# Laying a planned instruction order with 140 stored shifts of its due times

## The chip, the cores and the metric

One NeuronCore of a Trainium2 chip runs the whole program. The metric is the device time of one execution in microseconds (us). The program has five instruction queues that run on their own and meet through semaphores: TensorE (PE, with its weight loads as PEld), VectorE (DVE), ScalarE (ACT), GpSimd (POOL) and SyncE (SP), which here issues nearly all DMA transfers.

## The reference

One layer of a decoder with three groups of heads, 1024 tokens of 2048 channels, float32:

```python
h = rmsnorm(x, ln_g)
proj = h @ w_in                                   # columns split among the groups
(g_u, g_v, g_z, d_q, d_k, d_v, d_z, d_a, d_b, c_q, c_z) = split(proj)
out_a = gmlp_spatial_gating(g_u, g_v, ...) * silu(g_z)          # 4 groups of 128, chunks of 128
q, k, v = split(causal_conv_silu(concat(d_q, d_k, d_v)))
o = gated_delta_rule(l2norm(q), l2norm(k), v, g, beta)          # 8 heads of 128, chunked
out_b = rmsnorm(o, dn_norm_g) * silu(d_z)
mk, mv = split(rmsnorm(mem, mem_norm_g) @ w_mem_kv)             # 256 memory tokens
out_c = softmax(c_q @ mk.T / sqrt(128)) @ mv * silu(c_z)        # 4 heads of 128
x = x + concat(out_a, out_b, out_c) @ w_out
return rmsnorm(x, final_g)
```

## The kernel before, in words

Tokens are handled in two halves of 512, channels in 16 blocks of 128. The two large projections (into the heads, `project_stage`, and out of them, `out_pair`) are done as block products with seven instead of eight multiplications (`seven`): sums and differences of halves of the activations and of the weights are made first, and products are combined afterwards. Float32 accuracy comes from splitting each operand into a rounded high part and a remainder (`split_to`: a cast on ACT, a subtraction on DVE) and multiplying three times (`triple`). In the profile the high and low parts of the weights are `rhi` and `rlo`, those of the activations `lh` and `ll` or `lm`, loaded weights are `raw` and `kept`, PSUM banks are `acc` and `dn`, results copied out of them `obs`, `yu` and `yz`.

In order of time: the memory's keys and values are projected and `x` is normed and turned (to about 80 us); the head projections run from there to about 1250 us, and between their products lie the delta rule's convolution, inverse and scan (`front`, `inverse`, `levels`, `scan_step`), the spatial gating (`spatial`, `gmlp`) and the attention (`attend`); the output projection runs to the end, with the final norm in `close`.

None of this order is the order of the program text. Every call such as `PE.matmul` or `Q.dma_start` goes through an `Engine` and is stored by `Plan.add` as an `Op` with its engine, its estimated cost (`price`), the operations that must wait for it (`succ`) and a class from `rank(...)`. Classes under zero mark the first loads. PE operations given inside `together()` have one head, `lead`, and follow it as its `tail`. At the end `Plan.issue` decides the order and calls the stored functions in it, which puts them on the engines' queues. That is why the profile gives line 398, the call in `issue`, for every instruction.

Three functions make the order:

- `lay(key, hold)` plays the operations through a model of the engines. At each step the engine that is free first takes, among its ready operations, the one with the smallest key. It writes each operation's planned start into `o.at` and returns the planned end. DMA transfers go one after another at `DMA_RATE` bytes a nanosecond after the issue, and land `DMA_FIXED` nanoseconds later; SyncE may not run more than `AHEAD` nanoseconds ahead of them. On ACT an operation that needs another function table is put back by `hold`.
- `late(preds)` plays the same operations backwards from the last layout and returns for each the latest start (negative, counted back from the end) that still keeps the end, with distances lengthened by `STRETCH`. These are the keys, the deadlines, of the next `lay`.
- `issue` starts with the classes as keys, alternates `lay` and `late` for `PASSES` rounds, keeps the layout with the smallest planned end, sorts the operations by it and issues them.

Keys and times in the plan are nanoseconds.

Of the kernel before, what the change touches and what calls it, by code (L numbers as in the profile page):

```python
# [53 lines left out]
class Engine:  # L54
    def __init__(self, plan, eng, ns):
        self.plan, self.eng, self.ns = plan, eng, ns
# [6 lines left out]
class Plan:  # L63
# [3 lines left out]
    DMA_RATE = 350.0  # L67
    DMA_FIXED = 3800.0
    SWITCH = 250.0
    FIRST, SPREAD, PASSES, STRETCH, AHEAD = 0, 1.75, 8, 1.25, 1000.0  # L70
    TABLE, HOLD = 1300.0, 6000.0

    def __init__(self, nc):
        self.ops = []
# [247 lines left out]
    def late(self, preds):  # L322
# [56 lines left out]
                    heapq.heappush(soon[lead.eng], (ready[lead.idx], lead.idx))  # L379
        return goal  # L380

    def issue(self):
        preds = [[] for _ in self.ops]
        for o in self.ops:
            for s in o.succ:
                preds[s.idx].append(o)
        best = None
        key, hold = [o.cls for o in self.ops], 0.3
        for n in range(self.FIRST + self.PASSES + 1):
            end = self.lay([o.cls * 1.0e9 + o.idx if o.cls < 0 else k for o, k in zip(self.ops, key)], hold)  # L390
            if best is None or end < best[0]:
                best = end, [o.at for o in self.ops]
            key, hold = self.latest() if n < self.FIRST else self.late(preds), self.HOLD
        for o, o.at in zip(self.ops, best[1]):
            pass
        self.ops.sort(key=lambda o: (o.at, o.idx))
        for o in self.ops:
            o.fn(*o.args, **o.kw)  # L398
# [1523 lines left out]
```

## Time and profile before

| | |
|---|---|
| median of 3 runs | 1594.31 us (1592.87 to 1595.48) |
| the profiled execution's own time | 1593.81 us |
| its span, first to last instruction | 1592.1 us |
| instructions | 24568 |
| PE matmuls | 8349, busy 1570.2 us |
| DVE, ACT, POOL busy | 1228.7, 963.3, 106.7 us |
| mean granted PE clock | 0.997 |
| DMA | 434.12 MB, mean 273 GB/s |

Busy time counts the instructions' own time on an engine. Matmuls overlap each other, and their ends are modelled, so a PE that is busy all the time is not for that reason at its highest pace. Idle time of an engine matters only where the work that ends last waits for it. In the rows of stretches the columns are the stretch, its length, then busy time and, in brackets, number of instructions of PE, PEld, DVE, ACT and POOL, the granted clock of PE as a share, the mean busy share of the 16 DMA engines and what they moved.

### The profile page before, as it was taken

Reading aid. Unit: us, or ns where it says so; the run is one execution under the profiler, and the core shown is the slowest. Engines: PE = TensorE matmul, PEld = TensorE weight load, DVE = VectorE, ACT = ScalarE, POOL = GpSimd, SP = SyncE. Lnnn points to the kernel's source line nnn. Section 1 sums busy time; section 2 is a strip of 40 time slices with the busy share of each in tenths; the row PEclk is TensorE's granted clock in tenths of the full one; section 3 lists DMA queues with packets and bytes.
Section 4 is the critical chain, followed back from the end, with each engine's and each line's share of the span. In section 5 each row is a group of like instructions: output and inputs, shape, how many; then the busy total and the mean of one; then the engine's idle time right before and its main releaser. Section 6 shows DMA issues by size and latency. Waiting matters only on the chain.

```text
span 1592.1 us, 24568 instructions
## 1 busy us (share of the span) xinstructions
PE 1570.2 (99%) x8349; PEld 1315.3 (83%) x8349; DVE 1228.7 (77%) x1818; ACT 963.3 (61%) x2006; POOL 106.7 (7%) x143
## 2 busy tenths in 40 slices
PE   8999999999999999999999989999999999999997
PEld 7988888888887888888888878888888888888886
DVE  6977655877589997777789996867658888688875
ACT  6833255535698436787886557765658864344455
POOL 0100010001000100111111001000000000000001
PEclk9999999999999999999999999999999999999999
DMA  9999966888679898786888988999877989778647
GB/s 320 327 317 346 284 171 183 294 292 245 218 246 315 298 325 254 257 250 205 282 281 277 303 244 245 341 325 309 268 245 253 298 298 347 235 263 293 232 146 276
DMA packets 335951, 434.12 MB, mean 273 GB/s; under 512 B 70089, under 2 KB 160466, under 8 KB 335826
## 3 DMA queue, kind: packets, MB, share of 16 engines
q1 hardware_dynamic: 334098, 429.39, 83.3%
q0 software_dynamic: 1088, 2.10, 0.4%
q8 instruction: 66, 1.08, 0.3%
q10 hardware_dynamic: 640, 1.07, 0.2%
q14 instruction: 59, 0.48, 0.1%
HBM read 332.78 MB, written 99.16 MB: 271 GB/s over the span
## 4 chain that ended last, share of the span: by engine, by line
PE 92%; ACT 3%; DMA 2%; DVE 1%; issue 1%; SPq 0%; POOL 0%; POOLq 0%; ACTq 0%; DVEq 0%
PE acc L398 56%; PE dn L398 35%; ACT jk L398 1%; ACT rhi L398 1%; DMA h0d<-tn 1%; SPq L398 0%; DMA tn<-vd 0%; DMA ut<-in_x_dram 0%; DMA kept<-in_mem_dram 0%; DVE rlo L398 0%; DMA raw<-in_w_in_dram 0%; DVE vs L398 0%; ACT vs L398 0%; DVE tn L398 0%; ACT inv L398 0%
## 5 line engine op out<-in xcount | busy, mean ns | idle before, releaser
L398 PE MATMUL acc<-lh,rhi 128*128 128x512 f32 x1024 | 396.2, 396 | 2.9 <-DVE obs L398 1.2
L398 PE MATMUL acc<-lh,rlo 128*128 128x512 f32 x1024 | 382.9, 397 | 0.0
L398 ACT CAST rhi<-raw 128x1024 fp32r<-128x1024 f32 (+1 forms) x148 | 186.6, 1261 | 248.8 <-PE dn L398 133.8
L398 DVE TENSOR_TENSOR rlo<-raw,rhi 128x1024 fp32r<-128x1024 f32 (+1 forms) x148 | 219.3, 1482 | 109.0 <-ACT rhi L398 98.8
L398 PE MATMUL acc<-ll,rhi 128*128 128x512 f32 x688 | 268.0, 395 | 0.8 <-DVE ll L398 0.8
L398 PEld LDWEIGHTS acc<-lh,rhi 128*128 128x128 f32 x1024 | 192.3, 188 | 41.1 <-issue 1.5
L398 PEld LDWEIGHTS acc<-lh,rlo 128*128 128x128 f32 x1024 | 191.9, 188 | 37.4
L398 DVE TENSOR_TENSOR ll<-ll,lh 128x1024 fp32r<-128x1024 f32 x122 | 148.5, 1217 | 17.3 <-ACT lh L398 17.0
L398 PEld LDWEIGHTS acc<-ll,rhi 128*128 128x128 f32 x688 | 129.6, 189 | 26.4 <-DVE ll L398 1.3
L398 ACT CAST lh<-ll 128x1024 fp32r<-128x1024 f32 x122 | 128.2, 1051 | 29.5 <-PE dn L398 9.0
L398 PE MATMUL acc<-lm,rhi 128*128 128x512 f32 x336 | 130.6, 394 | 0.0
L398 PE MATMUL dn<-lh,rhi 128*128 128x512 f32 x288 | 112.6, 393 | 0.0
L398 PE MATMUL dn<-lh,rlo 128*128 128x512 f32 x288 | 109.7, 393 | 0.0
L398 DVE TENSOR_TENSOR raw<-raw,kept 128x1024 f32<-128x1024 f32 (+1 forms) x56 | 80.9, 1444 | 6.9 <-DMA raw<-in_w_in_dram 5.9
L398 DVE TENSOR_TENSOR rlo<-kept,rhi 128x1024 fp32r<-128x1024 f32 (+1 forms) x29 | 41.8, 1443 | 47.3 <-ACT rhi L398 44.4
L398 PE MATMUL dn<-ll,rhi 128*128 128x512 f32 x192 | 75.2, 393 | 0.0
L398 PEld LDWEIGHTS acc<-lm,rhi 128*128 128x128 f32 x336 | 63.2, 188 | 11.9
L398 ACT CAST rhi<-kept 128x1024 fp32r<-128x1024 f32 (+1 forms) x29 | 35.6, 1229 | 50.3 <-PE dn L398 26.2
L398 PEld LDWEIGHTS dn<-lh,rhi 128*128 128x128 f32 x288 | 54.1, 188 | 10.6
L398 PEld LDWEIGHTS dn<-lh,rlo 128*128 128x128 f32 x288 | 54.0, 188 | 10.5
L398 POOL TENSOR_TENSOR hs<-hs,mhalf 128x4 f32<-128x4 f32 x32 | 48.4, 1515 | 195.3 <-DVE hs L398 194.9
L398 POOL TENSOR_TENSOR small<-small,mhalf 128x1 f32<-128x1 f32 x26 | 21.6, 832 | 562.8 <-DVE small L398 562.8
(421 smaller groups left out, 3449.6 us busy)
## 6 DMA issues: line engine op xcount, KB each, us to landing
raw<-in_w_in_dram SPq DMA_DIRECT2D x120, 512.0 KB
ll<-hsd SPq DMA_DIRECT2D x54, 512.0 KB
raw<-in_w_out_dram SPq DMA_DIRECT2D x48, 512.0 KB
raw<-in_w_in_dram SPq DMA_DIRECT2D x72, 256.0 KB
lm<-hsd SPq DMA_DIRECT2D x26, 512.0 KB
pd<-obs SPq DMA_DIRECT2D x48, 256.0 KB
late<-os SPq DMA_DIRECT2D x44, 256.0 KB
kept<-in_w_in_dram SPq DMA_DIRECT2D x20, 512.0 KB
```

The lines of the kernel that those rows point to most:

```text
L398: o.fn(*o.args, **o.kw)
```

## The change

`PASSES` goes from 8 to 16, so the loop in `issue` makes 17 layouts instead of 9 and keeps the best of them, now with its keys. These keys are then changed by `nudged`, and one more `lay` with the changed keys gives the order that is issued. `fixed` is what stood in the loop before: operations of a class under zero keep the key of their class.

`nudged` goes through the 140 stored numbers `NUDGES` in order. A number's top bits are its kind, the rest seeds a small generator (`draw`). Kind 0 picks a stretch of the kept layout (a start, and a length from `WIDTHS`), a reach from 256 to 32768 ns and a share, and adds to the key of that share of the stretch's operations a random amount of that scale, up or down. Kind 1 picks one operation and takes the reach off its key and off those of its ancestors that lie within half a width before it. Kind 2 picks one operation and adds the reach to its key and to those of its heirs within half a width after it. Heads of PE bundles stand for their bundles. The numbers were chosen beforehand, under layouts with late transfers; the kernel itself only applies them. No operation, buffer or dependency is added or removed.

```diff
-    FIRST, SPREAD, PASSES, STRETCH, AHEAD = 0, 1.75, 8, 1.25, 1000.0
+    FIRST, SPREAD, PASSES, STRETCH, AHEAD = 0, 1.75, 16, 1.25, 1000.0
     TABLE, HOLD = 1300.0, 6000.0
+    WIDTHS = (4.0e3, 8.0e3, 16.0e3, 24.0e3, 40.0e3, 60.0e3, 90.0e3, 140.0e3)
+    NUDGES = (
+        26298409, 11320507, 8404763, 7722074, 16576787, 19920401, 40970024, 17359656, 9019627,
...
+        10043970, 4847855, 34621008,
+    )
...
+    def fixed(self, key):
+
+        return [o.cls * 1.0e9 + o.idx if o.cls < 0 else k for o, k in zip(self.ops, key)]
+
+    def nudged(self, preds, end, at, key):
+
+        key = list(key)
+        heads = sorted((at[o.idx], o.idx) for o in self.ops if o.lead is o and o.cls >= 0)
+        for n in self.NUDGES:
+            kind, s = n >> 24, n & 0xFFFFFF
+
+            def draw():
+                nonlocal s
+                s = (s * 1664525 + 1013904223) & 0xFFFFFFFF
+                return s >> 8
+
+            draw(), draw()
+            if kind:
+                t0, i = heads[int(draw() / 2.0**24 * len(heads))]
+                width = 0.5 * self.WIDTHS[draw() >> 21]
+                reach = 2.0 ** (8 + (draw() >> 21))
+                seen, todo = {i}, [i]
+                while todo:
+                    o = self.ops[todo.pop()]
+                    key[o.idx] += -reach if kind == 1 else reach
+                    for x in (o, *o.tail):
+                        for q in preds[x.idx] if kind == 1 else x.succ:
+                            q = q.lead
+                            near = at[q.idx] > t0 - width if kind == 1 else at[q.idx] < t0 + width
+                            if q.idx not in seen and q.cls >= 0 and near:
+                                seen.add(q.idx)
+                                todo.append(q.idx)
+                continue
+            first = draw() / 2.0**24 * end
+            last = first + self.WIDTHS[draw() >> 21]
+            reach = 2.0 ** (8 + (draw() >> 21))
+            share = ((draw() >> 21) + 1) / 16
+            for t, i in heads[bisect.bisect_left(heads, (first, -1)) :]:
+                if t >= last:
+                    break
+                if draw() / 2.0**24 < share:
+                    key[i] += reach * (draw() + draw() + draw() - 1.5 * 2.0**24) / 2.0**23
+        return key
...
-            end = self.lay([o.cls * 1.0e9 + o.idx if o.cls < 0 else k for o, k in zip(self.ops, key)], hold)
+            end = self.lay(self.fixed(key), hold)
             if best is None or end < best[0]:
-                best = end, [o.at for o in self.ops]
+                best = end, [o.at for o in self.ops], key
             key, hold = self.latest() if n < self.FIRST else self.late(preds), self.HOLD
-        for o, o.at in zip(self.ops, best[1]):
-            pass
+        self.lay(self.fixed(self.nudged(preds, *best)), self.HOLD)
```

More of the change, by code (lines that the diff above doesn't have):

```diff
@@ L1 @@
+import bisect
 import heapq
```

14 rows, old and new, of the table NUDGES are left out of this document.

## The prediction

> **What bounds the kernel now.** The page comes first: shares of busy time, then the chain that ended last.
>
> ```profile
> span 1592.1 us, 24568 instructions
> PE 1570.2 (99%) x8349; PEld 1315.3 (83%) x8349; DVE 1228.7 (77%) x1818; ACT 963.3 (61%) x2006; POOL 106.7 (7%) x143
> PE 92%; ACT 3%; DMA 2%; DVE 1%; issue 1%; SPq 0%; POOL 0%; POOLq 0%; ACTq 0%; DVEq 0%
> ```
>
> TensorE (PE) is busy in 99% of the span and is 92% of the chain. The change adds no matmul and takes none away, so only time in which PE is not working at its pace can be won. 1592.1 less 1570.2 leaves 21.9 us idle. The second view says where: busy time of each engine by stretch (length, then PE, PEld, DVE, ACT, POOL, granted clock, DMA share, GB/s).
>
> ```profile
> core 0: us, PE busy (x) PEld busy (x) DVE busy (x) ACT busy (x) POOL busy (x), PEclk, DMA share, GB/s
> 0.00:2.90 2.90, 0.01 (x1) 0.04 (x1) 0.00 (x0) 1.19 (x1) 1.39 (x10) 1.00 0.28 62
> 2.90:12.00 9.10, 6.95 (x27) 5.53 (x28) 3.36 (x8) 4.08 (x9) 0.00 (x0) 1.00 0.87 274
> 12.00:64.00 52.00, 52.00 (x356) 47.66 (x355) 43.77 (x74) 45.65 (x97) 6.14 (x7) 1.00 1.02 351
> 64.00:80.00 16.00, 14.89 (x120) 13.98 (x120) 14.44 (x31) 12.59 (x30) 1.44 (x3) 1.00 1.00 308
> 80.00:440.00 360.00, 360.00 (x1649) 298.32 (x1648) 241.09 (x279) 165.23 (x253) 22.25 (x31) 1.00 0.83 261
> 440.00:520.00 80.00, 78.35 (x405) 64.75 (x404) 70.42 (x136) 72.68 (x221) 6.64 (x8) 1.00 0.88 285
> 520.00:880.00 360.00, 359.84 (x2150) 303.06 (x2149) 300.60 (x504) 242.85 (x624) 40.33 (x47) 1.00 0.83 269
> 880.00:919.00 39.00, 37.85 (x170) 31.14 (x168) 36.07 (x60) 19.72 (x25) 2.45 (x2) 1.00 0.95 296
> 919.00:934.00 15.00, 12.05 (x43) 8.97 (x44) 14.41 (x35) 7.53 (x10) 0.59 (x1) 0.89 0.97 289
> 934.00:1000.00 66.00, 65.21 (x416) 54.12 (x414) 49.22 (x81) 45.56 (x94) 8.49 (x12) 1.00 0.83 249
> 1000.00:1320.00 320.00, 319.94 (x1868) 270.20 (x1869) 247.95 (x365) 219.71 (x473) 11.47 (x15) 1.00 0.89 292
> 1320.00:1582.00 262.00, 262.00 (x1157) 216.91 (x1156) 204.34 (x248) 123.14 (x169) 4.41 (x7) 1.00 0.75 253
> 1582.00:1592.10 10.10, 1.11 (x5) 0.57 (x4) 3.06 (x6) 3.39 (x6) 1.08 (x2) 0.65 0.75 277
> ```
>
> Read each row as length less PE: 2.89, 2.15, 0, 1.11, 0, 1.65, 0.16, 1.15, 2.95, 0.79, 0.06, 0 and 8.99, together 21.9. The first two are the wait for the first loads, the last is the final rows' norm and stores. In between lie 7.87 us in five places. The third view names what PE waited for there (total, times, longest).
>
> ```profile
> PE dn L398 <- DMA y<-in_mem_norm_g_dram: 2.9, 1, 2.9
> PE dn L398 <- DVE raw L398: 1.6, 1, 1.6
> PE dn L398 <- DMA gr<-in_ln_g_dram: 1.3, 1, 1.3
> PE acc L398 <- DVE obs L398: 1.2, 1, 1.2
> PE acc L398 <- DVE ll L398: 0.8, 1, 0.8
> PE dn L398 <- DMA tn<-vd: 0.8, 1, 0.8
> PE acc L398 <- ACT yu L398: 0.8, 1, 0.8
> PE dn L398 <- DVE tn L398: 0.6, 1, 0.6
> ```
>
> Outside the start every one is a single event: VectorE (DVE) late with obs, raw and ll around 919 to 934, where it is busy 14.41 of 15 us; ScalarE (ACT) late with yu in 440 to 520, where it is busy 72.68 of 80; a reload of tn just before 1000. Neither engine lacks time in the whole, only there. That is what an order can mend: in 80 to 440 DVE has 119 us free and ACT 195.
>
> The worst place costs a second time.
>
> ```profile
> 926.00:930.00 4.00, 1.50 (x6) 0.85 (x6) 4.00 (x14) 1.05 (x1) 0.36 (x1) 0.96 1.01 247
> 930.00:933.20 3.20, 3.20 (x10) 2.55 (x10) 3.04 (x7) 1.05 (x1) 0.00 (x0) 0.51 0.96 330
> ```
>
> After PE had worked 1.50 of 4 us, its granted clock was 0.51 for 3.2 us. Over the 15 us row the clock is 0.89, so 0.11 by 15 = 1.65 us are lost while PE counts as busy. [...]
>
> **The change part by part.**
>
> *What runs on the chip.* Nothing is added. `issue`, `fixed`, `nudged` and `lay` run while the program is built; the same operations, buffers and dependencies come out, in another order on each queue. Compute work stays at 1570.2 us of PE, 1228.7 of DVE, 963.3 of ACT. One exception: an order can change how often ACT reloads its table.
>
> ```profile
> L398 ACT ACT_TABLE_LOAD x23 | 29.5, 1283 | 2.7 <-PEq L1908 1.7 <-DVE small L398 0.6
> ```
>
> Five loads more or fewer are 6.4 us of ACT, hidden while ACT is at 61%; in 440 to 520, with 7.3 us free, two more would still fit. I put 0.
>
> *Twice as many passes (8 to 16).* The loop keeps the pass with the lowest end by the planner's own reckoning, so the base may be another order altogether. The trace can't show it. Bounds: if no later pass is better, 0; otherwise anything that reordering can do, which is the next step's range.
>
> *The 140 nudges.* By their top bits 69 shift a stretch's operations at random, 45 pull an operation and its ancestors forward, 26 push an operation and its heirs back, by 256 to 32768 ns. Decoded with the generator in `nudged`, 14 of the 69 stretches begin in the first tenth of the plan, 32 between two and four tenths (about 320 to 640 us), 8 between five and six. So they stand densest where the rows show 1.11 and 1.65 us idle, thinner where 4.1 (1.15 and 2.95) are. Each moved operation takes its DMA issue along, and SyncE's queue works in order:
>
> ```profile
> SPq L398 <- PE dn L398: 203.7, 121, 5.4
> SPq L398 <- DVE rlo L398: 145.2, 90, 5.2
> SPq L398 <- PE acc L398: 122.3, 67, 4.9
> ```
>
> It waits anyway, up to 5.4 us at a time, for PE to free a buffer. A load put behind such a wait comes later, one put ahead earlier. POOL, busy 7%, hides its own moves.
>
> *What can be won.* The loads at the very start have a negative class, which `fixed` keeps as before: 2.89 and 2.15 stay. The last 8.99 is a chain of norm and stores behind the last matmul: stays. Left: 1.11 + 1.65 + 0.16 + 1.15 + 2.95 + 0.79 + 0.06 = 7.87 idle, plus 1.65 of half clock: 9.5 us. That is the upper end, since no row shows more; the lower end is a loss, as new stalls can open (priced below). Of the 9.5 I take 60%, 5.7: the DVE knot at 919 to 934 is the largest piece and has slack before it, but 14.41 of 15 us busy means that a whole stretch must move, not one operation. Where it goes, the next late thing is ACT's or DVE's casts in the same crowded stretches.
>
> *Sum.* The profiled execution took 1593.81 us (span 1592.1 plus 1.7 around it), 0.5 below the median 1594.31. 1593.81 - 5.7 = 1588.1; I say 1588.
>
> [...]
>
> **The rivals.** A difference of 0.2%, 3.2 us, is about what a measurement can tell from none.
>
> *A, the forecast (0.54):* the knots at 440 to 520 and 880 to 934 open mostly, nothing as large closes. Gains from 3.2 to 9.5: 1584 to 1591.
>
> *B, nothing to see (0.24):* the order mends what its plan shows, not what the chip does. The stalls are single events of under 1.7 us, and the nudges' densest stretches hold 1.11 and 1.65 idle: 2.8 us even if both go, so 1591 to 1597. Against it: the 4.1 us at 880 to 934 sit on DVE load, which a plan can see.
>
> *C, slower (0.18):* a weight load for the output projection (1320 to 1582, no idle now) slips behind waits of SyncE's queue. Each slip of its longest wait is 5.4 us of idle PE, plus half of 3.2 us at half clock, 1.6: 7.0. DVE has 58 us free there and can't make a late load good. One slip with A's gain of 5.7 gives 1595; it decides once losses exceed 5.7 + 3.2 = 8.9, so from two slips: 14.0 - 5.7 = 8.3, near 1602. Against it: DMA is at 0.75 in that stretch, and `lay` lets SyncE issue only while less than 1 us of transfers is queued (`AHEAD`), a rule that stays.
>
> *D, more than the idle (0.04):* time hidden in "busy" shrinks too. 12 to 64 is 52 us with no idle, yet DVE 43.77 and ACT 45.65 pace it and the chain runs through ACT and DVE there. If ACT's 45.65 set it alone, 6.4 us would go as well: 1593.8 - 9.5 - 6.4 = 1578.
>
> **How the numbers follow.** Forecast 1588, own range 1584 to 1591. The range for 8 in 10 takes in B whole and the lower part of C, down to beyond A's upper gain: 1580 to 1600. Faster is A + D, 0.58; the same is B, 0.24; slower is C, 0.18.
>
> **What would show it.** Right: PE busy within 3 us of 1570, span shorter, PE idle between 12 and 1582 us under 4; no wait of PE on DVE raw, obs or ll over 0.5 us; granted clock 1.00 throughout 12 to 1582. B: the idle total between 5 and 10, in other places. C: idle or a half clock in 1320 to 1582 on a DMA wait. Wrong altogether: a changed count of matmuls, or PE's busy time moving by more than its idle.

## The result and the profile after

The changed kernel takes 1585.74 us in the median of 5 runs (1582.74 to 1587.86), the kernel before 1594.31 (1592.87 to 1595.9, now 5 runs). The ratio is 0.9946, 95% interval 0.9934 to 0.9957: 8.6 us or 0.54% faster. The profiled execution took 1585.74 us and spans 1584.0, 8.1 less than before.

From the page of the changed kernel, span, busy time and the chain that ended last:

```profile
span 1584.0 us, 24571 instructions
PE 1568.0 (99%) x8349; PEld 1316.2 (83%) x8349; DVE 1229.7 (78%) x1818; ACT 965.3 (61%) x2004; POOL 98.5 (6%) x143
PE 98%; issue 0%; DMA 0%; DVE 0%; SPq 0%; ACT 0%; POOLq 0%; POOL 0%; DVEq 0%
```

The matmuls are as many as before. PE's idle time fell from 21.9 to 16.0 us (5.9 of the 8.1), its busy time from 1570.2 to 1568.0 (the other 2.2). The chain is now 98% PE.

The same stretches as before, of the changed kernel (the last two end 8 us earlier; those not shown, 12 to 64, 80 to 440 and 1000 to 1320, have no idle time of PE):

```profile
2.90:12.00 9.10, 6.56 (x23) 5.00 (x24) 3.56 (x9) 4.09 (x9) 0.00 (x0) 1.00 0.87 308
64.00:80.00 16.00, 16.00 (x137) 15.87 (x136) 15.90 (x30) 12.32 (x33) 1.48 (x2) 1.00 1.03 314
440.00:520.00 80.00, 80.00 (x408) 67.52 (x407) 73.68 (x127) 70.73 (x202) 7.20 (x9) 1.00 0.86 280
520.00:880.00 360.00, 359.74 (x2155) 303.20 (x2154) 303.73 (x518) 247.93 (x640) 33.43 (x46) 1.00 0.85 274
880.00:919.00 39.00, 39.00 (x177) 32.30 (x177) 37.77 (x64) 23.08 (x31) 2.03 (x2) 1.00 0.99 309
919.00:934.00 15.00, 15.00 (x73) 12.42 (x73) 14.21 (x35) 6.26 (x7) 1.71 (x2) 1.00 0.95 285
934.00:1000.00 66.00, 64.00 (x478) 53.34 (x477) 49.06 (x77) 45.56 (x100) 7.40 (x12) 0.98 0.83 239
1320.00:1574.00 254.00, 254.00 (x1123) 210.38 (x1122) 196.17 (x238) 117.23 (x157) 4.09 (x7) 1.00 0.76 251
1574.00:1584.00 10.00, 1.68 (x8) 1.07 (x6) 3.15 (x6) 3.40 (x6) 0.64 (x2) 0.82 0.78 285
```

Four of the five places with idle PE are clean: 64 to 80, 440 to 520, 880 to 919, 919 to 934. The fifth, 934 to 1000, has 2.00 us instead of 0.79. PE's waits say with what:

```profile
PE dn L461 <- DMA y<-in_mem_norm_g_dram: 2.9, 1, 2.9
PE acc L461 <- DVE ll L461: 2.0, 1, 2.0
PE dn L461 <- DMA gr<-in_ln_g_dram: 1.0, 1, 1.0
PE dn L461 <- DMA kept<-in_mem_dram: 0.9, 1, 0.9
```

Three of the four are first loads. The new one, DVE late with `ll`, stands at 994 to 996, and its origin is a load. Stretches of time there, then SyncE's issues (start, duration of so many issues), then DVE's instruction that waited:

```profile
980.00:984.00 4.00, 4.00 (x29) 3.65 (x29) 3.16 (x7) 1.48 (x4) 0.00 (x0) 1.00 0.40 97
992.00:996.10 4.10, 2.11 (x55) 1.24 (x53) 3.58 (x4) 3.04 (x8) 0.00 (x0) 1.00 1.08 391
996.10:999.60 3.50, 3.50 (x10) 2.73 (x11) 3.50 (x5) 2.36 (x5) 0.00 (x0) 0.60 1.00 310
```

```profile
972.10 3.79 SPq L461 DMA_DIRECT2D sm<-gvd  x4
975.99 4.13 SPq L461 DMA_DIRECT2D vd<-sm  x4
984.70 0.41 SPq L461 DMA_DIRECT2D raw<-in_w_in_dram  x1
992.52 1.23 DVE L461 TENSOR_TENSOR raw<-kept,raw 128x1024 f32<-128x1024 f32 x1 [4.47 <-DMA raw<-in_w_in_dram]
994.80 1.22 DVE L461 TENSOR_TENSOR ll<-ll,lh 128x1024 fp32r<-128x1024 f32 x1
```

SyncE spends 7.9 us from 972.1 on eight issues. In the 4 us behind them the DMA engines' share is down to 0.40. The weight load of 984.70 comes after these eight and eight more. DVE waits 4.47 us for the load, two operations of 1.2 us (`raw` and `rlo`) then stand ahead of `ll`, and PE is idle for 2.0 us. After it the granted clock is 0.60 for 3.5 us. In the kernel before, the half clock stood in 930 to 933.

**Where the time went, by equal work.** A row's idle time does not tell how fast PE is inside "busy". So I gave each matmul about the spacing that its shape shows in the trace where nothing holds it up (0.227 us for 512 columns, 0.105 for 128; the medians over either whole trace are 0.227 and 0.109), summed these in order of time, and compared when the two kernels reach equal sums. After minus before, for the stretches between these times of before:

| stretch of before | after minus before | its idle and half clock before |
|---|---|---|
| start to 20 us | +1.3 | 2.89 + 2.15 (first loads) |
| 50 to 90 | -2.2 | 1.11 |
| 90 to 440 | +0.3 | 0 |
| 440 to 520 | -3.2 | 1.65 |
| 520 to 880 | +0.1 | 0.16 |
| 880 to 950 | -6.9 | 1.15 + 2.95 + 1.65 of clock |
| 950 to 975 | -0.6 | part of 0.79 |
| 975 to 1015 | +3.2 | rest of 0.79 |
| 1015 to the last matmul | +0.6 | 0.06 |
| behind the last matmul | -0.7 | 8.99 |

Together -8.1. The three knots (50 to 90, 440 to 520, 880 to 950) gave 12.3 us, where their rows showed 8.5. The rest of the gain, 3.8, was slow pace counted as busy. The table is an estimate that hangs on the spacings: with the 1st to the 50th percentile of each shape's spacings in the two traces, the three knots come to 12.3 to 13.0, 440 to 520 alone to -3.1 to -3.9, and 975 to 1015 to 2.8 to 4.8.

The slow pace can also be seen without these weights. A matmul of 512 columns is drawn 0.39 us long, while the next one can start 0.227 us after it, so a short wait disappears under the modelled end of the matmul before it. The weight loads show such waits. Here are the longest of PEld's in 440 to 520 of the kernel before; they are 4.1 us in all, where PE's row shows 1.65 idle:

```profile
PEld acc L398 <- ACT yu L398: 1.2, 1, 1.2
PEld acc L398 <- ACT obs L398: 0.9, 2, 0.8
PEld dn L398 <- ACT os L398: 0.7, 1, 0.7
PEld dn L398 <- DVE ai L398: 0.5, 1, 0.5
```

The changed kernel has none there. Over 50 to 90, 440 to 520 and 880 to 934, the weight loads waited 11.8 us before (2.0 + 4.1 + 5.7) and not at all after; PE's rows showed 6.9 of it.

The 1.3 us lost at the start are 0.4 us of idle time and, for the larger part, pace: matmuls of 256 columns in a row start 0.21 us apart until 11.5 us in the kernel before and until 13.7 in the changed one, and 0.12 apart afterwards. Experiment 9, with the order of the kernel before there, changes pace at 10.3, so this point moves between executions.

### The profile page after: what moved, and what is told of

The parts are those of the page before. It is cut to its first block, busy times and chain, and to the rows that moved or that the text cites. A ratio compares the mean times of both kernels' runs of the same rounds, so it can differ in the third digit from the quotient of the medians.

```text
span 1584.0 us, 24571 instructions
## 1 busy us (share of the span) xinstructions
PE 1568.0 (99%) x8349; PEld 1316.2 (83%) x8349; DVE 1229.7 (78%) x1818; ACT 965.3 (61%) x2004; POOL 98.5 (6%) x143
## 4 chain that ended last, share of the span: by engine, by line
PE 98%; issue 0%; DMA 0%; DVE 0%; SPq 0%; ACT 0%; POOLq 0%; POOL 0%; DVEq 0%
PE acc L461 60%; PE dn L461 38%; DMA kept<-in_mem_dram 0%; SPq L461 0%; DVE rlo L461 0%; DVE ll L461 0%; ACT obs L461 0%; DVE kd L461 0%; DVE vs L461 0%; POOLq L1980 0%; POOL small L461 0%; DVE kT L461 0%; DVE small L461 0%; ACT sm L461 0%; DVEq L461 0%
## 5 line engine op out<-in xcount | busy, mean ns | idle before, releaser
L461 PE MATMUL acc<-lh,rhi 128*128 128x512 f32 x1024 | 390.1, 396 | 0.0
L461 PE MATMUL dn<-rlo,lh 128*128 128x512 f32 x144 | 56.1, 389 | 0.0
L461 PE MATMUL dn<-rhi,ll 128*128 128x512 f32 x144 | 56.1, 389 | 0.0
```

## The experiments

All kernels are compared with runs of the kernel before on the same chip (medians 1594.5 to 1595.6).

**1 and 2. The shifts applied to one part of the time only.** `nudged` returns the shifted keys before 550 us of the plan and the unshifted ones behind it, or the other way round.

```diff
-        key = list(key)
+        old, key = key, list(key)
...
-        return key
+        return [k if t < 550.0e3 else o for k, t, o in zip(key, at, old)]    # e1_early
+        return [k if t >= 550.0e3 else o for k, t, o in zip(key, at, old)]   # e2_late
```

> The nudges' shifts are kept only for operations that the kept layout starts before 550 us; the others have their old keys. Theory T (each knot is opened in its own place): the gains up to 560 us of the changed kernel stay (0.4 us lost at the start, 1.1 us idle gone at 64 to 80, 1.65 us idle and about 1.5 us of stretched pace gone at 440 to 520), about 3.7 us in all, and the knot at 880 to 934 is there as before (some 4 us idle and one half clock): 1589 to 1592 against 1594.3, span 3 to 5 us shorter. Rival U (the gain comes from the layout as a whole): the half alone gives nothing, within 2 us of before.

> The other half: shifts only for operations that the kept layout starts at or after 550 us. Theory T: PE idle at 440 to 520 stays at about 1.65 us and at 64 to 80 at 1.1, the knot at 919 to 934 (2.95 us idle, 1.65 us of half clock, 1.15 idle just before) is gone, 4 to 7 us, less 2 to 3.6 us if the new stall near 992 us comes with it: 1587 to 1591. Rival U: within 2 us of before.

The early half gives 1591.68 us, ratio 0.9987 (0.9976 to 0.9997), the late half 1593.3, 0.9989 (0.9979 to 0.9999): 2.8 and 1.2 us of the 8.6. But each half opens its own knots just as the whole does. Of the early half, two stretches:

```profile
440.00:520.00 80.00, 80.00 (x407) 67.44 (x406) 73.22 (x127) 70.80 (x202) 7.21 (x9) 1.00 0.86 280
520.00:880.00 360.00, 356.67 (x2140) 300.04 (x2140) 301.01 (x511) 245.84 (x640) 36.73 (x46) 1.00 0.84 270
```

By equal work it has -2.2 in 50 to 90 and -3.2 in 440 to 520, as the whole change has, and then +3.8 in 520 to 880, most of it in waits of PE between 640 and 760 (3.3 us). The late half keeps its knots before 550 and gains 5.2 at 880 to 950, then loses 3.3 and 2.4 behind 975. Its median fits the rival, within 2 us of before, and only its trace fits the theory. This trace has to be read with care: its execution took 1596.97 us, 3.7 over the median, and it also lost 3.0 us between 50 and 160, where PE's order is the same, matmul by matmul, as in the kernel before.

So the knots are untied locally, but the gain is not a sum of parts: behind 550 us, where shifted and unshifted keys meet, the early half has stalls in 520 to 880 (+3.8) that the full set has not (+0.1), and the late half loses more behind 975 (5.7) than the full set does (3.8). How much of the late half's loss is chance of one execution is not shown. The knots themselves repeat: idle time in 440 to 520 is 1.65 us before and 1.64 in the late half and in experiment 9, which have the same order there.

**3. The same kinds and number of shifts, from other seeds.**

```diff
-            kind, s = n >> 24, n & 0xFFFFFF
+            kind, s = n >> 24, (n + 3) & 0xFFFFFF
```

> The same 140 kinds, with 3 added to each seed, so other places and other shifts of the same spread of sizes. Theory T (the stored numbers fit the places that they were chosen for): shifts of up to 32 us put loads and splits past their deadlines, PE idle grows from 16 us to 40 or more, 20 to 45 us slower than before, 1615 to 1640, with waits of PE on DVE, ACT and DMA all over. Rival V (any shuffle of a tight layout loosens its knots): within 5 us of before, some knots gone and others new.

1637.78 us, ratio 1.0266 (1.0252 to 1.028), 43 us slower. Its largest wait of PE:

```profile
PE acc L461 <- ACT lh L461: 10.7, 9, 2.3
```

So the gain does not come from shuffling as such. Only one other set of seeds was tried. Whether a set unlike the 140 can gain as much is not shown: those of experiments 7 and 8 hold some 130 of the old numbers.

**4. The late load of 984.70.** Three SyncE operations that hold it up are laid behind it; the rest of the order stays.

```diff
         self.lay(self.fixed(self.nudged(preds, *best)), self.HOLD)
+        for n, i in enumerate((8651, 9013, 7710)):
+            self.ops[i].at = self.ops[9067].at + 1.0 + n
```

> The changed kernel, with one block moved on SyncE's queue alone: the weight load of raw that was issued at 984.70 us goes ahead of three issues that stood before it (a store of obs, a load of ll, a load of kT; 1 MB together). Theory T (the new stall at 992 to 996 us is SyncE's: its queue had fallen 4 us behind, at a DMA share of 0.40 in 980 to 984): the load lands 3 to 4 us earlier, DVE's wait of 4.5 us for it shrinks to under 1, PE's 2.0 us idle on ll goes and with it the half clock, 2 to 3.6 us less than the changed kernel, 1582 to 1584. Rival W (the transfers themselves are the limit there, share 1.00 and over in 984 to 996): the wait moves to ll, kT or tn, within 1 us of the changed kernel, PE idle in 984 to 1000 still 1.5 to 2.5.

1584.49 us, ratio 0.9933 (0.992 to 0.9947), which can't be told from the changed kernel. In the profile the wait on `ll` is gone and no half clock follows, but another 1.0 us of idle time opens (a stretch, SyncE's issues, DVE's instruction that had waited, PE's waits):

```profile
996.00:1000.00 4.00, 2.95 (x14) 2.19 (x14) 3.57 (x5) 3.56 (x8) 0.00 (x0) 1.00 1.06 385
```

```profile
976.78 4.55 SPq L463 DMA_DIRECT2D vd<-sm  x4
984.34 0.40 SPq L463 DMA_DIRECT2D raw<-in_w_in_dram  x1
989.19 1.22 DVE L463 TENSOR_TENSOR raw<-kept,raw 128x1024 f32<-128x1024 f32 x1
```

```profile
PE dn L463 <- issue: 1.3, 2, 1.0
```

The load is issued only 0.36 us earlier by the clock, because this execution is 1.4 us later at that place (the eight issues begin at 973.46 instead of 972.10). But it is there when DVE asks for it: DVE starts at 989.19 without a wait, 4.85 us after the issue, where the changed kernel's DVE got the load 7.82 us after the issue (984.70 to 992.52) and that of experiment 5 7.6 us after. So without the three transfers (1 MB) ahead of it the load is there some 3 us sooner after its issue. By equal work 975 to 1015 costs +1.4 over before instead of +3.2. So this load is the origin of the stall as far as one profile shows it; what it is worth in the median stays open, since the next run shows how much this place moves by itself.

**5. The changed kernel again, unaltered**, beside the next three.

> The changed kernel once more, unaltered, so that the other three of this group are compared with it on one chip. Every theory: 0.4 to 0.7% under the kernel before, about 1585.7; PE idle between 12 and 1574 us near 2.3, the wait on ll near 992 to 996 there again.

1584.93 us, 0.9941 (0.9929 to 0.9952). Its profiled execution, the slowest of the five (1587.74), shows the same instructions in other stalls: PE is idle for 4.59 us between 12 and 1574, not the 2.3 that was expected (PE's waits, then the stretches at 992 to 1000):

```profile
PE acc L461 <- DVE ll L461: 2.1, 2, 1.7
PE acc L461 <- ACT yu L461: 1.3, 1, 1.3
```

```profile
992.00:996.00 4.00, 3.40 (x61) 2.30 (x59) 2.48 (x3) 3.56 (x10) 0.07 (x1) 1.00 1.10 377
996.00:1000.00 4.00, 2.60 (x10) 1.80 (x11) 4.00 (x5) 2.50 (x7) 0.00 (x0) 1.00 1.01 317
```

The stall on `ll` is there again, with DVE waiting 4.13 us for the same load but no half clock behind it, and 1.3 us of `yu` appear behind it. The three knots are as in the first profile: -2.2, -3.2 and -6.4. A difference of 1 to 2 us in one place of one profile is therefore no evidence, while the knots, which repeat, are.

**6. One shift of the 140 left out**, the last, of the kind that pushes an operation and its heirs back.

```diff
-        10043970, 4847855, 34621008,
+        10043970, 4847855,
```

> The changed kernel without the last of its 140 nudges; the plan's own end goes from 1572.3 to 1581.3 us, the difference lying at 430 to 570 us. Theory T (a nudge has its worth only with all others in place, as each later layout hangs on every earlier choice, and the chip follows the plan): the gain at 440 to 520 goes or a new wait of 2 to 6 us opens at 520 to 600; 3 to 9 us slower than the changed kernel, 1588 to 1594. Rival X (the plan's stalls at 430 to 570 are for the most part its own, since the kernel before ran past 1.9 us of them at 560): within 2 us of the changed kernel.

1592.33 us, 0.9987 (0.9979 to 0.9996): 7.4 us slower than the changed kernel on the same chip, for one number. Stretches, and PE's longest waits between 400 and 620:

```profile
440.00:520.00 80.00, 79.09 (x403) 66.36 (x402) 72.20 (x121) 70.77 (x204) 3.71 (x6) 1.00 0.89 284
520.00:880.00 360.00, 358.02 (x2137) 299.57 (x2136) 300.39 (x510) 244.22 (x630) 37.55 (x48) 1.00 0.84 270
919.00:934.00 15.00, 15.00 (x72) 12.47 (x71) 15.00 (x32) 8.21 (x11) 0.59 (x1) 1.00 1.02 315
```

```profile
PE dn L461 <- DVE lm L461: 1.0, 1, 1.0
PE acc L461 <- DVE ll L461: 0.9, 2, 0.8
PE dn L461 <- ACT os L461: 0.9, 1, 0.9
```

The knots at 50 to 90 and 880 to 950 stay untied (-2.1, -6.9), but 90 to 440 takes 1.3 us more than in the changed kernel, 440 to 520 1.4 and 520 to 880 3.4. By equal work all of it, some 6 us, arises between 400 and 600. So the last shift closes small waits for ACT and DVE that the other 139 leave there.

**7 and 8. More shifts, chosen to bear lateness better**: 330 and 352 numbers in `NUDGES` in place of 140, most of the old ones among them, nothing else altered.

> The changed kernel with 330 nudges instead of 140, most of the new ones picked so that the issued order loses less when transfers land late and SyncE's issues take longer; the plan's own end stays (1572.6 for 1572.3). Theory R (of the plan's 15.5 us the chip gave 8.1 in the profile, because transfers and issues came later than planned, above all at 992): PE idle between 12 and 1574 us under 1, no half clock there, 2 to 5 us under the changed kernel, 1580.5 to 1584. Rival Y (what is left is pace and the plan's own pessimism in the kernel before, not lateness): within 1.5 us of the changed kernel.

> As the one before, with another set of 352 nudges, picked in the same way from other draws; the plan's own end is 1572.3. Theory R: the same gain, 2 to 5 us under the changed kernel, since it is the slack against lateness that counts and not these numbers. Rival Y: within 1.5 us of the changed kernel. If one of the two sets gains and the other doesn't, neither holds as stated, and the difference is in single stalls.

1587.39 us, 0.9953 (0.9941 to 0.9965), and 1587.1, 0.9949 (0.9937 to 0.996). No gain over the changed kernel (1584.93); the intervals overlap. PE's idle time between 12 and 1574 us is 2.67 (the row below) and 2.72, where the changed kernel had 2.27 and 4.59 in two executions:

```profile
12.00:1574.00 1562.00, 1559.33 (x8320) 1307.52 (x8320) 1223.17 (x1804) 954.79 (x1990) 93.80 (x132) 1.00 0.85 274
```

The theory expected less than 1 us idle, and that did not come about either. So these two sets did not pay; whether lateness still costs something in the changed kernel is not settled by them.

**9. The worst knot by itself.** In the kernel before, without any shift, four products on DVE at 925.87 to 928.24 (`raw` from `dn` times `utri`), for which PE waited 1.65 us, are laid together ahead of the 1.2 us subtraction for `rlo` that came before them.

```diff
         for o, o.at in zip(self.ops, best[1]):
             pass
+        for n, i in enumerate((7356, 7357, 7358, 7359)):
+            self.ops[i].at = self.ops[8709].at - 1.0 + 0.1 * n
```

> The kernel before, with one edit on DVE's queue alone: the four products raw<-dn,utri, on which PE waited 1.65 us at 928.30, stand together ahead of the 1024-wide split that came before them, as they stand together in the changed kernel. Theory K (the order of these four was the knot): PE's wait on DVE raw goes, and with less idle the half clock at 929.7 to 933.1 too; PE idle in 919 to 934 falls from 2.95 to about 1.3, 1.6 to 3.3 us less than before, 1591 to 1593. Theory S (the knot is a stretch: DVE is 14.41 of 15 us busy there, and the matmul behind these waits for ll, which DVE can't give before 929.6 us as long as ACT's cast of lh begins only at 926.28): the wait moves to ll and grows to 2.5 to 3.5 us, PE idle in 919 to 934 stays between 2.3 and 3.5, within 1 us of before.

1594.62 us, 0.9996 (0.9987 to 1.0005): no change. The profile shows where it went. Of this kernel, the four products on DVE, the cast on ACT and the subtraction on DVE that make `ll`, PE's wait, the stretch:

```profile
923.38 0.85 DVE L400 TENSOR_TENSOR raw<-dn,utri 128x128 f32<-128x128 f32 x4
924.14 1.22 DVE L400 TENSOR_TENSOR rlo<-raw,rhi 128x1024 fp32r<-128x1024 f32 x1
926.09 1.05 ACT L400 CAST lh<-ll 128x1024 fp32r<-128x1024 f32 x1 [2.05 <-DMA ll<-hsd]
927.89 1.22 DVE L400 TENSOR_TENSOR ll<-ll,lh 128x1024 fp32r<-128x1024 f32 x1
929.17 0.79 PE L400 MATMUL acc<-ll,rhi 128*128 128x512 f32 x1 [3.32 <-DVE ll L400]
919.00:934.00 15.00, 11.57 (x42) 8.93 (x41) 14.60 (x34) 6.87 (x10) 0.59 (x1) 0.81 0.95 286
```

The first product comes 2.5 us earlier and the last 4.0, and PE's wait for them is gone. PE then waits 3.32 us for the next thing, `ll`, which starts at 927.89 where it started at 928.37. So this one place in DVE's queue was not the knot. (The half clock behind the stall lasts 6.8 us in this execution, 3.4 in that of before.)

It was not DVE's queue alone either. The subtraction needs ACT's cast, and the cast waited 2.05 us for the load of `ll` and ended at 927.14; DVE's own queue then held `ll` back for 0.75 us. By these rows some 2.6 of the 3.32 us would have stayed with an idle DVE (an estimate). DVE's busy share says the same: experiment 6 has DVE busy for 15.00 of 15 us in 919 to 934, and PE too. What differs around the knot is what ACT, which makes the casts, waits for in 900 to 934. First the longest of its waits for loads before, then its longest waits after:

```profile
ACT lh L398 <- DMA lm<-hsd: 2.7, 1, 2.7
ACT lh L398 <- DMA ll<-h0d: 2.0, 1, 2.0
ACT rhi L398 <- DMA raw<-in_w_in_dram: 1.8, 1, 1.8
ACT rhi L461 <- PE acc L461: 9.9, 3, 3.7
ACT lh L461 <- PE acc L461: 6.0, 3, 3.5
```

Before, ACT's casts wait for loads, 6.9 us in all. In the changed kernel they wait for PE to be done with a buffer, 15.9 us, and for weights or activations not at all. So the chain of load, cast and subtraction runs ahead of PE there. That this is what opened the knot is a reading of the waits; no run moved these loads by themselves.

## Why the prediction was right, and where not

The forecast, 1588.0 with 1584 to 1591 as its own range, held: 1585.74. Rival A was the case. Step by step:

- *Nothing is added on the chip*: right. The number of matmuls is the same, and DVE's and ACT's busy times agree within 2 us. The table loads fell from 23 to 21, with no effect to be seen, as said:

```profile
L461 ACT ACT_TABLE_LOAD x21 | 26.9, 1283 | 2.4 <-PEq L1971 1.7 <-DVE small L461 0.4
```

- *Twice as many passes, 0 if no later pass is better*: that case. Printed while the program is built, the pass with the lowest planned end is one of the first nine; with the 140 shifts, 8 passes give the same order on every queue, instruction by instruction. The bound was right and the whole effect is the shifts'.
- *What can be won, 9.5 us at most, "since no row shows more"*: the net gain, 8.1 to 8.6, stayed under it, but the reason failed. The three knots alone gave some 12.3 (8.5 by their rows). A row's idle time leaves out the slow pace beside it: PE counts as busy on matmuls that are fed slower than they could run. That is rival D's mechanism, put at 4 in 100 and in the wrong place: 12 to 64 us shrank by nothing, 440 to 520 and 880 to 950 did.
- *60% of it*: wrong as a share, and that it came out near the truth was luck, because two errors cancelled. The knots opened wholly, not by 60%, and 3.2 + 1.3 + 0.6 us of new losses at 975 to 1015, the start and behind 1015 took a part back. The sum said -5.7; the profile -8.1.
- *A whole stretch must move, not one operation*: that the four products were not enough is shown by experiment 9 (0.9996). The reason given, DVE busy for 14.41 of 15 us, does not hold: with DVE at 15.00 of 15, experiment 6 has no idle PE there. The loads ahead of ACT's casts, which the prediction left out, were late too.
- *The next late thing is a cast or subtraction on ACT or DVE in a crowded stretch*: right in kind (`ll` at 994), though behind it stood a load.
- *The start and the end stay*: nearly. The first loads cost 5.4 us idle for 5.0 (by equal work the start cost 0.4 to 1.4 more than before in the profiles of the changed order, mostly by the later change of pace), the end 8.32 for 8.99.
- *Rival C, a load slipping on SyncE's queue*: it happened once, in the head projections and not in the output projection, and cost 2.0 us idle and a half clock, not 7.0. It could not decide the sign.
- *Rival B*: wrong about this chip. The plan's ends are 1587.8 before and 1572.3 after, a planned gain of 15.5 of which 8.6 arrived; experiments 3 and 6 were planned at +34 and +9.0 against their bases and came out at +43 and +7.4. The plan has the direction right and the size off, too large twice and too small once.
- *Signs*: PE busy within 3 us of 1570 (1568.0) came true, and so did PE idle under 4 us in the middle (2.27 in 12 to 1574, as the last matmul now comes 7.4 us earlier), though the second execution had 4.59. "No wait on raw, obs or ll over 0.5 us" and "granted clock 1.00 throughout" did not: 2.0 us on `ll` and 0.60 for 3.5 us, both at the one new stall.

On the clock, the half-clock stretch is as long as before, 3.4 us in both profiles, and follows a stall again: 2.11 us of work in 4.10. The longest single wait of PE ahead of it was 2.0 us here and 1.65 us before. In the unaltered repeat, PE works 3.40 and 2.60 of 4 us at the same place and the clock stays 1.00. A stall of that size does not always bring it either: in experiment 1 PE works 12.35 of 15 us in 919 to 934, and in experiment 2 it waits 2.5 us for `ll`, both at clock 1.00. So what the prediction read in the kernel before, 1.50 us of work in 4 and then a clock of 0.51, holds for that one execution. What sets the clock these runs do not show.

What stays open: how much the late load at 984.70 is worth in the median, and whether the loads, DVE's queue or both opened the knot at 880 to 934. For the knots at 64 to 80 and 440 to 520 the waits that went are shown, but no run tells what in the order removed them.

## What to carry to other kernels

When the engine that bounds a kernel is 99% busy, look for the few places where it waits for single late results, and look at the weight loads' waits as well as at its own idle rows: here the places gave 12.3 us, where the idle rows and the half clock showed 8.5. New losses elsewhere took 4 us of that back, so such a sum is not yet a forecast. Moving the one operation that was waited for only handed the wait to the next one (experiment 9); follow that one back to its loads before calling an engine's queue the cause. This order, tuned as a whole, could not be taken apart: half of the shifts gave 2.8 or 1.2 us of 8.6, and leaving out one number of 140 lost 7.4. So each variant must be measured, and single stalls of 1 to 2 us in one profile must not be read as its effect.

## What the runs showed that was not expected

- One order has different stalls in different executions: the changed kernel's waits between 12 and 1574 us were 2.0 + 0.3 us in one profile and 2.1 + 1.3 + 0.6 + 0.3 + 0.2 in the other, and PE's last matmul came 7.4 and 5.4 us earlier than before.
- SyncE took 3.79 us for four issues of 64 KB (`sm` from `gvd`), 4.13 and 4.55 for four of `vd` from `sm` in two profiles, about 1 us each, where the weight load of 984.70 takes 0.41. Behind eight of them in a row the DMA engines' share is 0.40, at 97 GB/s. This holds for these places only: over the whole trace the median issue of `sm` from `gvd` takes 0.64 us and that of `vd` from `sm` 0.43.
